# The layer-0 input stage of a two-layer trunk: pooled pieces stored one hook later, and two kinds of stores issued by another engine

## The chip, the cores and the metric

One core of a Trainium2 chip runs one program. The metric is device time in microseconds (us): the median of several executions. A profile is one execution of its own, recorded by the hardware profiler; its times are us from the first instruction.

## The reference, cut to what matters

The program is one inference step of a trunk of two layers on 2048 sample tokens and 128 context tokens of width 1024. Layer 0 modulates and normalises the tokens, projects them into six parts, and mixes two branches:

```python
q_lat, kv_lat, k_pe, gate_a, pool_in, gate_b = jnp.split(h @ w_in, SPLITS_AB, axis=-1)
q = (rmsnorm(q_lat, q_norm) @ w_uq).reshape(B, T, MLA_HEADS, QK_NOPE + QK_ROPE)
...
for g, w in enumerate(POOL_WINDOWS):      # 2, 4, 8, 16 tokens, four groups of 128 channels
    mean = (csg[:, hi] - csg[:, lo]) / (hi - lo)
    d = mean - uf[:, :, sl]
    outs.append(d @ w_pool[g])
o_b = jnp.concatenate(outs, axis=-1) * pool_scale
mixed = jnp.concatenate([o_a * jax.nn.silu(gate_a), o_b * jax.nn.silu(gate_b)], axis=-1)
```

The change touches only how the pooling branch and the q products are carried through memory in layer 0's input stage.

## The kernel before

**Stages.** The input stage of layer 0 is the first quarter of the program (about 60 to 500 us), then come attention and the rest. It walks over five blocks of tokens (512, 512, 512, 384 and 256 wide, blocks 0 to 4). Per block, TensorE (PE) makes products against pairs of weight tiles: `kv` (one pair), `q` (one pair), then `pool`, `gb` and `ga` (two pairs each; block 0 has `gb`, `ga`, `pool`). A pair fills one of two PSUM buffers `psA`, so PE cannot start the pair after next before the buffer is read out.

**Weights.** `wload` (L421 to L424) loads a raw tile `r` from memory by a transfer that SP issues, ScalarE (ACT) casts it to the high part (L423), and VectorE (DVE) subtracts for the low part (L160). Every product is three matmuls (L177 to L179). A `w` in a row is such a tile; four raw tiles exist at a time.

**Evacuation.** `evac_consume` reads a finished pair with one ACT activation (L592, SiLU or copy) and stores it by `store_pair` to `up_d`, `gb_d` or `ga_d` in memory; `store` (one line, L167 in the trace) picks the issuing queue by a letter: 's' is SP, 'a' ACT. The q products are split by an ACT cast (L562, high part, stored by `ST_QH`) and a DVE subtract (low part, `ST_QL`) into `q_d`; the rope part (L492 to L495 on DVE, cast L579) goes out by `ST_QP`.

**Hooks.** After each pair of `pool`, `gb` and `ga` the program writes a hook: one step of each of some generators. 'n' prepares the next block (L333, L295, then L357 and L351 on DVE and L361 on ACT: the modulated tokens `h`), 'l' is a quarter of the modulation vector (four L266 on DVE, from a raw tile `r` of `w_ada_T` by SP), 'p' is a step of the pooling of the block before.

**Pooling.** For each of four channel groups (`gi` 0 to 3) `pool_sums` loads `u` from `up_d` and `gt` from `gb_d` into tiles `pl` (four buffers in all), POOL (GpSimd) makes the window sums (L640, then L644 up to three times for `gi` 3), and `gate` scales on DVE (L654, L656) and stores to `mix_d` (by SP). Before, one hook step is the gate and the store of one group, and at once the loads and sums of the next.

**Order.** Each engine and each queue runs its instructions in the order in which the program writes them, as far as the framework's scheduler leaves it. A load on SP that waits for a buffer holds everything behind it on SP.

Of the kernel before, what the change touches and what calls it, by code (L numbers as in the profile page):

```python
# [65 lines left out]
POOL_AT = 0  # L66
POOL_Y = 0
ST_POOL = 's'
ST_EV = 's'
ST_QH = 's'  # L70
ST_QL = 's'
ST_QP = 's'
ST_X = 'g'
# [40 lines left out]
def trunk_kernel(ctx, tc, xT, cols_in, cond_in, ident_in, edge_in, rope_in, w_ada, w_ada_T, w_in_t, w_inp_T, w_pool,  # L114
# [41 lines left out]
    def f(ap):  # L156
        return ap.bitcast(F32)
# [8 lines left out]
    def store(c, *a):  # L166
        qs[c].dma_start(*a)  # L167
# [39 lines left out]
    mix_d = dram.tile([8, P, T], F32, name="mix_d")  # L207
# [325 lines left out]
    def q_consume(bi, ps, tab):  # L533
# [19 lines left out]
        for hp in range(2):  # L553
# [11 lines left out]
            for a in range(2):  # L565
                store(ST_QH, q_d[2 * hp + a, :, 0, o:o + n], f(th[:, a, :n]))
                store(ST_QL, q_d[2 * hp + a, :, 1, o:o + n], f(tl[:, a, :n]))
# [17 lines left out]
    def store_pair(dst, i, o, n, t):  # L585
        store(ST_EV, dst[i:i + 2, :, o:o + n].rearrange("g p n -> p g n"), t[:, :, :n])

# [22 lines left out]
    def pooling(t0, t1, lo_t, hi_t, alloc=pool_tiles, size=PT):  # L610

        m = -(-(t1 - t0) // size)
        cuts = [t0 + (t1 - t0) * i // m for i in range(m + 1)]
        for a, b in zip(cuts[:-1], cuts[1:]):
            yield from pool_piece(a, b, lo_t, hi_t, alloc)

    def pool_piece(t0, t1, lo_t, hi_t, alloc):
        for gi in range(4):
            gate = pool_sums(gi, t0, t1, lo_t, hi_t, alloc)
            yield  # L620
            gate()
            if POOL_Y:
                yield

    def pool_sums(gi, t0, t1, lo_t, hi_t, alloc):

        w = WINDOWS[gi]
        n = t1 - t0
        L = n + 16
        u, gt, cur, other = alloc()  # L630
        a, b = max(t0 - 8, lo_t), min(t1 + 8, hi_t)
        c0 = a - (t0 - 8)
        if c0:
            G.memset(u[:, :c0], 0.0)
        c1 = c0 + b - a
        if c1 < L:
            G.memset(u[:, c1:L], 0.0)
        store(LD_POOL, u[:, c0:c1], up_d[gi, :, a:b])
        store(LD_POOL, gt[:, :n], gb_d[gi, :, t0:t1])
        G.tensor_tensor(out=cur[:, 1:L], in0=u[:, 0:L - 1], in1=u[:, 1:L], op=ALU.add)  # L640
        a0, a1, step = 1, L, 1
        while 2 * step < w:
            b0, b1 = a0 + step, a1 - step
            G.tensor_tensor(out=other[:, b0:b1], in0=cur[:, b0 - step:b1 - step],  # L644
                            in1=cur[:, b0 + step:b1 + step], op=ALU.add)
            cur, other = other, cur
            a0, a1, step = b0, b1, 2 * step
        if t0 == lo_t:
            G.tensor_tensor(out=cur[:, 8:16], in0=cur[:, 8:16], in1=edge[:, gi, 0:8], op=ALU.mult)
        if t1 == hi_t:  # L650
            G.tensor_tensor(out=cur[:, n:n + 8], in0=cur[:, n:n + 8], in1=edge[:, gi, 8:16], op=ALU.mult)

        def gate():
            V.scalar_tensor_tensor(out=cur[:, 8:8 + n], in0=cur[:, 8:8 + n], scalar=1.0 / w,  # L654
                                   in1=u[:, 8:8 + n], op0=ALU.mult, op1=ALU.subtract)
            V.scalar_tensor_tensor(out=cur[:, 8:8 + n], in0=cur[:, 8:8 + n],  # L656
                                   scalar=cols[:, C_PS + gi:C_PS + gi + 1],
                                   in1=gt[:, :n], op0=ALU.mult, op1=ALU.mult)
            store(ST_POOL, mix_d[4 + gi, :, t0:t1], cur[:, 8:8 + n])
        return gate  # L660

    def head_loads():
        uq, uk, up = ht(F32, (P, 4, 256)), ht(F32, (P, 4, P)), ht(F32, (P, 2, 2, P))
# [593 lines left out]
    def last_pooling():  # L1257
        todo = []
        for t0, t1, lo_t, hi_t in ((BLOCKS[-1][0] - 8, DEC, 0, DEC), (DEC, T, DEC, T)):
            for gi in range(4):  # L1260
                todo.append(pool_sums(gi, t0, t1, lo_t, hi_t, pool_tiles_late))
                if len(todo) > 2:
                    todo.pop(0)()
                yield
        for gate in todo:
            gate()
    pools = last_pooling()
    finishing = []
    g.gated = None
# [159 lines left out]
```

## Time and profile before

| | |
|---|---|
| median of 3 runs | 2059.51 us (2058.22 to 2059.84) |
| the profiled execution | 2053.45 us, of which 2051.7 us is the span |
| PE busy | 1986.3 us, 97% of the span, mean granted clock 0.993 |
| DVE, ACT, POOL busy | 1467.2, 1108.1, 581.3 us |

The profiled execution is 6.06 us below the median of the runs, so sums are made against 2053.45 us and carried over to the median as a difference. PE is busy nearly all the time; what can be gained or lost is in its 65 us of waits and in the stretches in which its clock is low.

### The profile page before, as it was taken

How to read it: one execution, taken by the hardware profiler on the slowest of the kernel's cores; microseconds unless marked ns; L12 is line 12 of the kernel's file. 1: busy time of each engine (PE TensorE's matmuls, PEld its weight loads, DVE VectorE, ACT ScalarE, POOL GpSimd, SP SyncE). 2: the span in 40 equal slices, each digit the busy share in tenths (PEclk: the TensorE clock that was granted, in tenths of full speed). 3: DMA queues.
4: the chain of work that ended last, by engine and by line, in shares of the span. 5: the costliest groups of instructions: out<-in, count | busy, mean ns of one | idle time of the engine just before them, and what ended most of it. 6: DMA issues, size and time to landing. Idle time of an engine off the chain costs nothing.

```text
span 2051.7 us, 26144 instructions
## 1 busy us (share of the span) xinstructions
PE 1986.3 (97%) x9652; PEld 1661.7 (81%) x9652; DVE 1467.2 (72%) x2222; ACT 1108.1 (54%) x1301; POOL 581.3 (28%) x405
## 2 busy tenths in 40 slices
PE   6999898999999999999999999999999999999997
PEld 3787787998777777777758788888889888889987
DVE  4698887765888888888884997455665566577575
ACT  4644344544676767676754635442454335535554
POOL 1002111111478787878762110001001110010000
PEclk9999999999999999999999999999999999999999
DMA  9587777676111010101135553344434542464463
GB/s 362 186 271 244 259 219 244 193 240 195 51 32 52 27 51 29 49 30 49 36 125 174 184 206 124 123 136 152 164 100 137 184 148 89 134 226 154 131 228 124
DMA packets 123696, 300.62 MB, mean 147 GB/s; under 512 B 12144, under 2 KB 39088, under 8 KB 123568
## 3 DMA queue, kind: packets, MB, share of 16 engines
q1 hardware_dynamic: 105168, 258.58, 38.2%
q10 hardware_dynamic: 13728, 23.60, 3.7%
q0 software_dynamic: 4672, 16.78, 2.3%
q8 instruction: 76, 1.25, 0.3%
q14 instruction: 52, 0.43, 0.1%
HBM read 243.23 MB, written 55.67 MB: 146 GB/s over the span
## 4 chain that ended last, share of the span: by engine, by line
PE 78%; DVE 9%; DMA 4%; issue 3%; ACT 3%; POOL 1%; SPq 1%; DVEq 0%; ACTq 0%; POOLq 0%
PE psA L177 17%; PE psA L178 17%; PE psA L179 17%; PE psA L821 3%; PE psA L822 3%; PE psA L823 3%; PE psA L824 3%; PE psA L825 3%; PE psB L178 2%; PE psB L179 2%; PE psB L177 2%; PE psB L917 2%; DVE w L160 1%; DMA r<-wp_d 1%; PE psB L1173 1%
## 5 line engine op out<-in xcount | busy, mean ns | idle before, releaser
L177 PE MATMUL psA<-h,w 128*128 128x512 f32 (+2 forms) x1600 | 578.3, 362 | 17.8 <-ACT e L592 16.1
L179 PE MATMUL psA<-h,w 128*128 128x512 f32 (+2 forms) x1600 | 574.0, 359 | 0.0
L160 DVE TENSOR_TENSOR w<-r,w 128x1024 fp32r<-128x1024 f32 x280 | 351.8, 1260 | 296.3 <-PE psA L178 199.8
L178 PE MATMUL psA<-h,w 128*128 128x512 f32 (+2 forms) x1536 | 550.0, 358 | 1.1 <-DVE h L160 1.1
L423 ACT CAST w<-r 128x1024 fp32r<-128x1024 f32 x280 | 291.9, 1049 | 253.2 <-PE psA L179 172.8
L177 PEld LDWEIGHTS psA<-h,w 128*128 128x128 f32 x1600 | 303.7, 190 | 58.8 <-ACT e L592 17.9
L179 PEld LDWEIGHTS psA<-h,w 128*128 128x128 f32 x1600 | 303.5, 190 | 38.3 <-issue 0.2
L178 PEld LDWEIGHTS psA<-h,w 128*128 128x128 f32 x1536 | 291.9, 190 | 37.7 <-DVE h L160 2.2
L874 POOL TENSOR_TENSOR w<-h,w 128x1024 fp32r<-128x1024 f32 x105 | 252.4, 2417 | 104.6 <-ACT w L872 101.3
L846 DVE TENSOR_TENSOR run<-psA,run 128x512 f32<-128x512 f32 x240 | 163.8, 683 | 42.1 <-ACT h L836 38.3
L836 ACT COPY h<-psA 128x1024 f32<-128x1024 f32 (+1 forms) x145 | 139.4, 962 | 78.2 <-PE psA L825 78.0
L868 ACT ACTIVATE h<-h 128x1024 f32<-128x1024 f32 (+1 forms) x145 | 143.4, 1011 | 64.0 <-DVE h L866 63.8
L866 DVE TENSOR_TENSOR h<-h,psC 128x1024 f32<-128x1024 f32 (+1 forms) x145 | 163.7, 1147 | 0.7 <-PE psC L860 0.7
L178 PE MATMUL psA<-o,w 128*128 128x512 f32 (+2 forms) x368 | 134.0, 366 | 0.0
L887 POOL TENSOR_TENSOR e<-e,h 128x512 f32<-128x512 f32 x92 | 120.8, 1313 | 5.3 <-ACT h L868 0.5
L872 ACT CAST w<-h 128x1024 fp32r<-128x1024 f32 x105 | 110.5, 1052 | 4.1 <-PE psB L179 3.1
L179 PE MATMUL psA<-o,w 128*128 128x512 f32 (+2 forms) x304 | 109.1, 361 | 0.0
L177 PE MATMUL psA<-o,w 128*128 128x512 f32 (+2 forms) x304 | 108.9, 361 | 0.0
L177 PE MATMUL psA<-w,h 128*128 128x512 f32 x272 | 106.7, 393 | 1.6 <-ACT o L1149 1.6
L640 POOL TENSOR_TENSOR pl<-pl 128x527 f32<-128x527 f32 (+2 forms) x16 | 18.8, 1177 | 308.7 <-DMA pl<-up_d 227.1
L178 PE MATMUL psA<-w,h 128*128 128x512 f32 x272 | 106.0, 390 | 0.1
L179 PE MATMUL psA<-w,h 128*128 128x512 f32 x272 | 105.9, 390 | 0.0
(298 smaller groups left out, 3543.2 us busy)
## 6 DMA issues: line engine op xcount, KB each, us to landing
r<-in_w_inc_t_dram SPq DMA_DIRECT2D x80, 512.0 KB, 3.5
r<-in_w_in_t_dram SPq DMA_DIRECT2D x60, 512.0 KB, 4.3
r<-in_w_oap_t_dram SPq DMA_DIRECT2D x40, 512.0 KB, 3.5
r<-in_w_incv_t_dram SPq DMA_DIRECT2D x40, 512.0 KB, 4.2
r<-in_w_outc_t_dram SPq DMA_DIRECT2D x40, 512.0 KB, 3.4
r<-in_w_ada_T_dram SPq DMA_DIRECT2D x32, 512.0 KB, 4.4
r<-wp_d SPq DMA_DIRECT2D x20, 512.0 KB, 5.6
h<-in_w_ada_dram SPq DMA_DIRECT2D x16, 512.0 KB, 10.2
```

Source lines behind the costliest of these rows:

```text
L160: eng.tensor_tensor(out=out, in0=a, in1=f(hi), op=ALU.subtract)
L177: PE.matmul(ps, w[0], x[0], start=first, stop=False)
L178: PE.matmul(ps, w[0], x[1], start=False, stop=False)
L179: PE.matmul(ps, w[1], x[0], start=False, stop=last)
L423: S.copy(hi, raw)
L836: S.copy(s[:, :nt], ps[:, :nt])
L846: V.tensor_tensor(out=b.max, in0=ps[:, a], in1=s[:, 0] if p == 0 else b.max, op=ALU.max)
L866: V.tensor_tensor(out=s[:, :nt], in0=s[:, :nt], in1=b.m[:, None, :].broadcast_to([P, nt, QB]), op=ALU.subtract)
L868: S.activation(out=s[:, :nt], in_=s[:, :nt], func=AF.Exp, scale=SM_SCALE)
L872: S.copy(ph[:, :nt], s[:, :nt])
L874: low = behind(G.tensor_tensor(out=pl[:, :nt], in0=s[:, :nt], in1=f(ph[:, :nt]), op=ALU.subtract), g.gated)
L887: behind(G.tensor_tensor(out=b.pool[:, 0], in0=b.pool[:, 0], in1=s[:, a], op=ALU.add), low or g.gated)
```

## The change

`ST_EV` and `ST_QH` go from 's' to 'a': the 30 stores of evacuated pairs and the 20 stores of q high parts are issued by ACT and no longer by SP (SP then has 601 rows in place of 651). And a group's pooling is in three steps: sums, gate, store. The store of a group, and with it the loads and sums of the next group, comes one hook behind its gate. What `drain(pools)` finds left at a block's end runs there. `last_pooling`, the pooling of the last tokens, calls the gate and the store together as before.

```diff
@@ -66,8 +66,8 @@
 POOL_AT = 0
 POOL_Y = 0
 ST_POOL = 's'
-ST_EV = 's'
-ST_QH = 's'
+ST_EV = 'a'
+ST_QH = 'a'
 ST_QL = 's'
 ST_QP = 's'
 ST_X = 'g'
@@ -616,11 +616,11 @@
 
     def pool_piece(t0, t1, lo_t, hi_t, alloc):
         for gi in range(4):
-            gate = pool_sums(gi, t0, t1, lo_t, hi_t, alloc)
+            gate, out = pool_sums(gi, t0, t1, lo_t, hi_t, alloc)
             yield
             gate()
-            if POOL_Y:
-                yield
+            yield
+            out()
 
     def pool_sums(gi, t0, t1, lo_t, hi_t, alloc):
 
@@ -656,8 +656,7 @@
             V.scalar_tensor_tensor(out=cur[:, 8:8 + n], in0=cur[:, 8:8 + n],
                                    scalar=cols[:, C_PS + gi:C_PS + gi + 1],
                                    in1=gt[:, :n], op0=ALU.mult, op1=ALU.mult)
-            store(ST_POOL, mix_d[4 + gi, :, t0:t1], cur[:, 8:8 + n])
-        return gate
+        return gate, lambda: store(ST_POOL, mix_d[4 + gi, :, t0:t1], cur[:, 8:8 + n])
 
     def head_loads():
         uq, uk, up = ht(F32, (P, 4, 256)), ht(F32, (P, 4, P)), ht(F32, (P, 2, 2, P))
@@ -1260,10 +1259,12 @@
             for gi in range(4):
                 todo.append(pool_sums(gi, t0, t1, lo_t, hi_t, pool_tiles_late))
                 if len(todo) > 2:
-                    todo.pop(0)()
+                    for it in todo.pop(0):
+                        it()
                 yield
-        for gate in todo:
-            gate()
+        for its in todo:
+            for it in its:
+                it()
     pools = last_pooling()
     finishing = []
     g.gated = None
```

The diff says little of where the rows end up, so three places are shown. The first is SP's queue in block 1, while the sums of that block's last group run (`r` from `in_w_in_t` are weights, from `in_w_ada_T` modulation; `e` evacuated tiles; `pl` pooling tiles). Before:

```order
L167 DMA r341_1748<-in_w_ada_T_dram 128x1024
L167 DMA pl320_1631<-gb_d_100 128x504
L167 DMA mix_d_102<-pl301_1530 128x504
L167 DMA pl423_2161<-up_d_99 128x528
L167 DMA up_d_99<-e315_1610 128x2x512
L421 DMA r346_1758<-in_w_in_t_dram 128x1024
L421 DMA r349_1764<-in_w_in_t_dram 128x1024
```

Now the same weights, there r346 and r349, are r342 and r345:

```order
L421 DMA r320_1625<-in_w_in_t_dram 128x1024
L167 DMA mix_d_102<-pl298_1518 128x504
L167 DMA pl334_1720<-gb_d_100 128x504
L167 DMA pl376_1957<-up_d_99 128x512
L421 DMA r323_1631<-in_w_in_t_dram 128x1024
L167 DMA r337_1730<-in_w_ada_T_dram 128x1024
L167 DMA pl377_1958<-gb_d_100 128x504
L421 DMA r342_1740<-in_w_in_t_dram 128x1024
L421 DMA r345_1746<-in_w_in_t_dram 128x1024
```

The load of pl423, which belongs to the next piece, stood directly ahead of the weights and is now eight rows behind them (it follows r385); the two `up_d` stores are on ACT.

The second place is DVE where block 0 ends: L266 of the modulation tile r251, w234 and w237 are weights, e241 the square sums of the next block. Before:

```order
L160 TENSOR_TENSOR w234_1220<-r232_1216,w233_1218 128x1024
L656 SCALAR_TENSOR_TENSOR pl258_1319<-pl258_1319,cols_81,pl257_1318 128x504
L160 TENSOR_TENSOR w237_1226<-r235_1222,w236_1224 128x1024
L160 TENSOR_TENSOR e241_1281<-e240_1279,e241_1281 128x512
L266 SCALAR_TENSOR_TENSOR psB252_1309,asum_96<-r251_1307,silb0_748 128x512
L266 SCALAR_TENSOR_TENSOR psE254_1313,asum_96<-r251_1307,silb1_749 128x512
L266 SCALAR_TENSOR_TENSOR psB253_1311,asum_96<-r251_1307,silb2_750 128x512
L333 TENSOR_TENSOR e246_1292<-e246_1292,e247_1294 128x1024
L266 SCALAR_TENSOR_TENSOR psE255_1315,asum_96<-r251_1307,silb3_751 128x512
```

Now:

```order
L266 SCALAR_TENSOR_TENSOR psB252_1309,asum_96<-r251_1307,silb0_748 128x512
L266 SCALAR_TENSOR_TENSOR psE254_1313,asum_96<-r251_1307,silb1_749 128x512
L160 TENSOR_TENSOR e202_1100<-e201_1095,e202_1100 128x512
L160 TENSOR_TENSOR w234_1220<-r232_1216,w233_1218 128x1024
L266 SCALAR_TENSOR_TENSOR psB253_1311,asum_96<-r251_1307,silb2_750 128x512
L266 SCALAR_TENSOR_TENSOR psE255_1315,asum_96<-r251_1307,silb3_751 128x512
L654 SCALAR_TENSOR_TENSOR pl258_1319<-pl258_1319,pl256_1317 128x504
L656 SCALAR_TENSOR_TENSOR pl258_1319<-pl258_1319,cols_81,pl257_1318 128x504
L160 TENSOR_TENSOR w237_1226<-r235_1222,w236_1224 128x1024
L160 TENSOR_TENSOR e241_1281<-e240_1279,e241_1281 128x512
L333 TENSOR_TENSOR e246_1292<-e246_1292,e247_1294 128x1024
```

All four L266 of r251 have moved from behind the row of e241 to ahead of it. On SP the load of r251 went from behind the q_d stores, rope and token loads to ahead of them.

The third place is DVE where block 2 ends: pl620 (before) and pl644 (now) are the gates of group 2, pl636 and pl678 those of group 3, L492 to L495 rope, and w554 and w557 the low weights of the two tiles of block 3's kv pair. Before:

```order
L160 TENSOR_TENSOR w554_2822<-r552_2818,w553_2820 128x1024
L654 SCALAR_TENSOR_TENSOR pl620_3181<-pl620_3181,pl618_3179 128x512
L656 SCALAR_TENSOR_TENSOR pl620_3181<-pl620_3181,cols_81,pl619_3180 128x512
L492 STREAM_SHUFFLE e541_2776<-e540_2774 128x512
...
L494 TENSOR_TENSOR e543_2788<-e543_2788,e398_2058 128x512
L160 TENSOR_TENSOR w557_2828<-r555_2824,w556_2826 128x1024
L495 TENSOR_TENSOR e543_2788<-e543_2788 128x512
L654 SCALAR_TENSOR_TENSOR pl636_3277<-pl636_3277,pl633_3274 128x512
L656 SCALAR_TENSOR_TENSOR pl636_3277<-pl636_3277,cols_81,pl634_3275 128x512
```

Now:

```order
L654 SCALAR_TENSOR_TENSOR pl644_3363<-pl644_3363,pl642_3361 128x512
L656 SCALAR_TENSOR_TENSOR pl644_3363<-pl644_3363,cols_81,pl643_3362 128x512
L160 TENSOR_TENSOR w554_2819<-r552_2815,w553_2817 128x1024
L654 SCALAR_TENSOR_TENSOR pl678_3592<-pl678_3592,pl675_3589 128x512
L656 SCALAR_TENSOR_TENSOR pl678_3592<-pl678_3592,cols_81,pl676_3590 128x512
L492 STREAM_SHUFFLE e537_2762<-e536_2760 128x512
...
L494 TENSOR_TENSOR e539_2774<-e539_2774,e398_2058 128x512
L160 TENSOR_TENSOR w557_2825<-r555_2821,w556_2823 128x1024
L495 TENSOR_TENSOR e539_2774<-e539_2774 128x512
```

The gate of group 3 stood behind the whole rope and w557 and is now ahead of both. The end of block 3 reads in the same way (pl785 ahead of the rope and of w684, where pl749 stood behind them). In block 2 itself the gate of group 3 (rows 291 and 296 of DVE's order, in the run between L333 and L357) is now at rows 264 and 274, where that of group 2 was.

## Rows read from the trace of the kernel before

**Rows 1.** waits of PE, 60 to 500 us: us in total, times, longest

```profile
PE psA L177 <- ACT e L592: 16.1, 4, 6.2
```

**Rows 2.** timeline of PE's four waits: start, length, operation, [idle before <-releaser]

```profile
184.75 0.47 PE L319 MATMUL psD<-e,ones 128*128 128x512 f32 x1 [2.11 <-DVE e L295]
...
218.78 0.80 PE L177 MATMUL psA<-h,w 128*128 128x512 f32 x1 [6.23 <-ACT e L592]
...
324.39 0.79 PE L177 MATMUL psA<-h,w 128*128 128x512 f32 x1 [6.17 <-ACT e L592]
...
414.27 0.68 PE L177 MATMUL psA<-h,w 128*128 128x384 f32 x1 [3.41 <-ACT e L592]
```

**Rows 3.** windows of 2 us of PE: length, busy (matmuls), granted clock, DMA share, GB/s

```profile
218.00:220.00 2.00, 1.22 (x3) 0.50 0.51 198
220.00:222.00 2.00, 2.00 (x7) 0.50 1.02 380
222.00:224.00 2.00, 2.00 (x8) 0.71 0.90 277
224.00:226.00 2.00, 2.00 (x11) 1.00 0.95 349
```

**Rows 4.** timeline of SP's queue behind the pooling store, block 1

```profile
198.23 0.33 SPq L167 DMA_DIRECT2D mix_d<-pl  x1
207.09 0.32 SPq L167 DMA_DIRECT2D pl<-up_d  x1
...
207.98 2.25 SPq L421 DMA_DIRECT2D r<-in_w_in_t_dram  x2
```

**Rows 5.** timeline of POOL, ACT and DVE in the same place

```profile
202.87 4.19 POOL L644 TENSOR_TENSOR pl<-pl 128x517 f32<-128x517 f32 x3 [3.13 <-DMA mix_d<-pl]
...
214.11 1.04 ACT L423 CAST w<-r 128x1024 fp32r<-128x1024 f32 x1 [3.89 <-DMA r<-in_w_in_t_dram]
...
217.70 1.02 ACT L592 ACTIVATE e<-psA 128x1024 f32<-128x1024 f32 x1
...
211.85 1.40 DVE L357 SCALAR_TENSOR_TENSOR h<-h,amul,e 128x512 f32<-128x512 f32 x2
```

**Rows 6.** timelines of SP and DVE ahead of it, block 0's end

```profile
145.64 7.82 SPq L167 DMA_DIRECT2D q_d<-e  x8
...
156.75 0.70 SPq L167 DMA_DIRECT2D r<-in_w_ada_T_dram  x1
...
165.51 0.70 DVE L266 SCALAR_TENSOR_TENSOR psB<-r,silb 128x512 f32<-128x512 f32 x1 [2.24 <-DMA r<-in_w_ada_T_dram]
```

**Rows 7.** timelines of ACT and DVE ahead of the second wait, block 2

```profile
320.86 1.14 ACT L361 ACTIVATE h<-h,mod 128x384 fp32r<-128x384 f32 x2 [1.58 <-DVE h L357]
...
303.28 0.63 DVE L654 SCALAR_TENSOR_TENSOR pl<-pl,pl 128x512 f32<-128x512 f32 x1
...
307.55 0.75 DVE L656 SCALAR_TENSOR_TENSOR pl<-pl,cols,pl 128x512 f32<-128x512 f32 x1
```

**Rows 8.** timelines of DVE, POOL and PE where blocks 2 and 3 end

```profile
356.91 0.75 DVE L656 SCALAR_TENSOR_TENSOR pl<-pl,cols,pl 128x512 f32<-128x512 f32 x1
...
364.31 2.07 DVE L160 TENSOR_TENSOR w<-r,w 128x1024 fp32r<-128x1024 f32 x1
...
362.45 5.09 POOL L644 TENSOR_TENSOR pl<-pl 128x525 f32<-128x525 f32 x3
...
364.73 0.33 PE L177 MATMUL psA<-h,w 128*128 128x384 f32 x1
364.90 0.34 PE L178 MATMUL psA<-h,w 128*128 128x384 f32 x1
```

**Rows 9.** landings of the pooling store, an issue on ACT, busy us in 100 to 500

```profile
mix_d<-pl SPq DMA_DIRECT2D x8, 256.0 KB, 3.5
...
554.94 0.35 ACTq L167 DMA_DIRECT2D e<-ga_d  x1
...
sum 400.00, PE 381.59 PEld 334.79 DVE 310.09 ACT 183.19 POOL 53.19; mean PE 95.40 PEld 83.70 DVE 77.52 ACT 45.80 POOL 13.30
```

## The prediction

> **What bounds the kernel now.** I read the page first: PE is busy 97% of the span, so only its waits and its slow-clock stretches can pay or cost. Everything that the change touches lies in layer 0's input stage, so next came the waits of PE there [rows 1] and PE's timeline at them [rows 2]. The reader is to see four waits and one kind: PE waits 6.23 us at 218.78, 6.17 at 324.39 and 3.41 at 414.27 for the activation L592 that empties `psA`, once in each of blocks 1 to 3, and 2.11 us at 184.75 for DVE's L295. That is 17.9 us. Behind each the granted clock is at its lower level: 0.50, 0.50 and 0.71 in three windows of 2 us behind the first, with 7 and 8 matmuls where 11 fit at 1.00 [rows 3]. Seven matmuls lost, at 2/11 us each, are 1.3 us. So about 1 to 1.5 us goes with a wait; for all four some 5 us. The most that the stage can give is 23 us, 1.1% of the time.
>
> Then the question for each wait is what its L592 waited for.
>
> *First wait.* ACT runs in order. L592 at 217.70 stands behind a table load, two L361 and the weight cast L423, which began at 214.11 after 3.89 us of waiting for its load of `r` [rows 5]. That load left SP at 207.98, behind a pooling load of `u` issued at 207.09 [rows 4]. SP's last issue before that was at 198.23, so it stood 8.5 us: the buffer came free only when POOL had ended three L644, begun at 202.87 and 4.19 us long, because they themselves wait for the landing of the store of 198.23 [rows 4, 5]. But DVE limits the same place: L361 needs L357, and the pair of L357 of 211.85 ends at 213.25 [rows 5]. From the cast's end (215.15) to L592 two L361 and a table load take 2.55 us. Had the weights been there, these would have run from 213.25, and L592 at 215.8 in place of 217.70. So SP alone is worth 1.9 us here; the rest hangs on DVE.
>
> *Second wait.* At 320.86 ACT waits 1.58 us for L357, no load is in it [rows 7]: DVE alone sets it. The third wait has the same form.
>
> **The change part by part.**
>
> *Weights ahead of the pooling load, block 1.* The order of SP shows the `u` load that stood for 8.5 us (pl423) behind the weights. The store of a piece, and the sums that wait for it, come a hook later. That gives the 1.9 us above.
>
> *The modulation load at block 0's end.* It left SP at 156.75 because eight q_d stores, which occupy SP's queue for 7.82 us, stood ahead, and an `up_d` store and others behind them; DVE then waited 2.24 us for it at 165.51 [rows 6]. Now it is ahead of the q_d stores. The four L266 (0.70 each and what follows: 2.6 us) leave the stretch in which DVE has no gap, and the wait goes with them, though some of the 2.24 us is taken up by the square sums' own inputs. I take 3.0 of the 4.8 us. DVE then ends L357 at 210.2, L592 can run at 212.8, and the wait falls by 1.9 + 3.0 to 1.3 us: **-5.0**, rounded, and with it the low clock's share of the place, **-1.2** (bounds: -2.5 if little of DVE's gain arrives, -7.5 if all of wait and clock goes). The wait of 2.11 us before it has DVE's same lateness and I give it **-0.8** (0 to -2.1).
>
> *Block 2.* A gate moves out of DVE's dense run ahead of L592: L654 and L656, 0.63 and 0.75 us [rows 7]; the stretch begins a little earlier because SP has one store fewer ahead of its weights, some 0.8 us. **-2.2** (-1.0 to -3.5). Block 3 has no gate in that run in either order: 0.
>
> *The gate of group 3 ahead of the rope, blocks 2 and 3.* This is the price. Before, the gate of group 2 ended at 357.66, the rope and the low weights of w557 followed, ending at 366.38, and the sums of group 3 ran beside them (three L644, 5.09 us). PE's kv pair began at 364.73, its matmuls stand 0.17 us apart, so its second tile, which needs w557, begins 24 matmuls later at 368.9 [rows 8]: 2.5 us to spare. Now DVE stands at the gate of group 3 with rope and w557 behind it. That gate needs the store of group 2 landed (3.5 us [rows 9]) and three L644. In block 1 such a three took 4.19 us [rows 5]. So from the end T of the gate of group 2: 0.2 + 3.5 + 4.2 + 1.4 for the gate itself, then 6.8 for rope and w557 without POOL beside them (8.7 before, an estimate from the seven rope rows at 0.7 and a subtract at 1.2, plus gaps), which makes T + 16.1 against 368.9. T can be 357.7 as before, and w557 is 4.9 us late; or as early as 352.7 or so, since the gates are now spread over more hooks, and nothing is late. I take T near 354, 1.0 us late, and 1.0 for the clock. Block 3 has the same order with narrower tiles; I take the same. Sum **+4.0**, bounds 0 and +13 (twice 4.9 and 1.5).
>
> *The issues on ACT.* 50 stores; one issue on ACT took 0.35 us, which makes 17.5 us spread over 440 us on an engine that is busy 45.8% there [rows 9]. Each follows the activation that made its data, so it waits for little; the cast behind it is what could be late, and the L592 of the three waits has no store ahead of it in its run. **0** (to +2 if a store stands for its semaphore ahead of a cast that matters).
>
> Sum: -5.0 - 1.2 - 0.8 - 2.2 + 4.0 + 0 = -5.2 us. From 2053.45 us that is 2048.3 us; the median of the runs lies 6.06 us above the profiled execution, so the forecast is 2059.5 - 5.2 = **2054.3 us**. A measurement tells about 0.2% from no change, 4.1 us, so this is faster by a little more than can be told.
>
> The Trainium skill (DMA: Bandwidth & Descriptors, Issuing engines are not separate DMA queues) says that transfers issued by several engines run on the same 16 DMA engines, so that spreading the issues saves only the sequencer's time. This trace agrees on the size of an issue (0.35 us on ACT, 0.32 on SP). What it doesn't cover is the 8.5 us that a load stood, which is a matter of order in one queue.
>
> **The rivals.**
>
> *No change: only issue time is saved.* The stores leave SP, but SP isn't what the L592 wait for: blocks 2 and 3 wait for L357 on DVE [rows 7], and in block 1 DVE's own limit lies 1.9 us below. If DVE doesn't start earlier, -1.9 and -1.4 for one gate, with the new gate order at +2, leave -1.3: 2058.2 us. For it: three of four waits end with DVE. Against it: DVE's wait of 2.24 us sits behind an SP queue that the change empties. Taken to its end, the rule of the Trainium skill named above (same page and section) gives this case too, at 2059.5 us.
>
> *A trade.* The four gains come, and the gate of group 3 is late by 3 us in each of two blocks, with 1.5 of clock: -9.2 + 9.0, 2059.3 us. Same by measurement, by another way.
>
> *Slower: DVE stands behind POOL at the kv pairs.* T stays at 357.7 in block 2 and as late in block 3, w557 comes 4.9 us late, 6.4 with the clock; if POOL is as slow as beside a busy DVE (5.09 in place of 4.19) 7.3. Twice 7.3 less 9.2 is +5.4: 2064.9 us. It decides from 6.7 us a place on (13.3 in all). For it: DVE's row order is certain. Against it: DVE idles before the old gates of groups 1 and 2, so T has room to come earlier.
>
> **How the numbers follow.** Forecast as above (faster, between 2048 and 2055.4): 0.47. The trade, with its neighbours: 0.16; no change: 0.13, so 0.29 within 0.2%. Slower: 0.24. The range reaches from all of the first waits' gains with no price, -9.2 and some more clock, 2048.5, to the slower rival, 2065.0; what is left out on each side is about one in ten. The forecast's own range is 2048.5 to 2057.
>
> **What would show it.** In the profile after: the wait at 218.78 at 1 to 3 us with ACT's cast there not waiting for a load; DVE's 2.24 us wait for the modulation tile gone; SP's 8.5 us stand no longer ahead of weights; the wait at 324.39 near 4 us, that at 414.27 unchanged. New: DVE idle 5 us or more at L654 with POOL's L644 as releaser at the ends of blocks 2 and 3, and perhaps waits of PE for DVE's w near 369 and 448. If those PE waits exceed 5 us each the prediction is wrong to the slow side; if DVE reaches the first L357 no earlier than before, it is wrong because the gain never was SP's.

## The result, and the profile after

The changed kernel takes 2069.1 us (median of 6 runs, 2064.84 to 2071.23) against 2058.86 us beside it: a ratio of 1.0055, 95% interval 1.0042 to 1.0068 (the two medians alone give 1.0050, inside it). It is slower. The forecast was 2054.3 us with a range to 2065.0, so the time lies outside the range, on the other side of no change.

The page of the changed kernel (busy us, share of the span, instructions):

```profile
span 2069.5 us, 26128 instructions
...
PE 1993.9 (96%) x9652; PEld 1665.6 (80%) x9652; DVE 1463.0 (71%) x2222; ACT 1109.7 (54%) x1301; POOL 580.6 (28%) x405
```

No engine has more work to speak of. Its waits of PE in 60 to 500 us (in total, times, longest):

```profile
PE psA L177 <- ACT e L592: 14.3, 5, 4.9
PE psD L319 <- DVE e L295: 5.0, 2, 3.8
PE psB L701 <- DMA e<-in_w_inp_T_dram: 4.5, 3, 2.3
PE psA L179 <- DVE w L160: 2.7, 3, 1.4
PE psD L320 <- DVE e L160: 1.8, 1, 1.8
```

The waits for L592 fell from 16.1 us in four [rows 1] to 14.3 in five. The others grew, and their places are in PE's timeline:

```profile
105.59 1.13 PE L701 MATMUL psB<-pl,e 128*128 128x128 f32 x8 [1.80 <-DMA e<-in_w_inp_T_dram]
118.12 0.50 PE L177 MATMUL psA<-h,w 128*128 128x512 f32 x1 [2.54 <-ACT e L592]
180.59 0.50 PE L179 MATMUL psA<-h,w 128*128 128x512 f32 x1 [1.38 <-DVE w L160]
192.55 0.47 PE L319 MATMUL psD<-e,ones 128*128 128x512 f32 x1 [1.23 <-DVE e L295]
223.70 0.79 PE L177 MATMUL psA<-h,w 128*128 128x512 f32 x1 [4.94 <-ACT e L592]
288.98 0.50 PE L320 MATMUL psD<-e,ones 128*128 128x512 f32 x1 [1.76 <-DVE e L160]
304.17 0.47 PE L319 MATMUL psD<-e,ones 128*128 128x512 f32 x1 [3.82 <-DVE e L295]
335.10 0.69 PE L177 MATMUL psA<-h,w 128*128 128x512 f32 x1 [3.27 <-ACT e L592]
380.12 0.44 PE L179 MATMUL psA<-h,w 128*128 128x384 f32 x1 [0.50 <-DVE w L160]
425.93 0.45 PE L177 MATMUL psA<-h,w 128*128 128x384 f32 x1 [3.29 <-ACT e L592]
460.79 0.39 PE L179 MATMUL psA<-h,w 128*128 128x256 f32 x1 [0.80 <-DVE w L160]
```

The rows at 192.55, 223.70, 335.10 and 425.93 answer to the four of [rows 2]: 1.23 for 2.11, 4.94 for 6.23, 3.27 for 6.17, 3.29 for 3.41. The rows at 380.12 and 460.79 are the kv pairs of the forecast's price.

Both programs issue the same matmuls in the same order (but for 23 rows near 100 us, where sixteen L701 and seven rows of the next pair have changed places), so the n-th of one trace can be held against the n-th of the other. I call the difference of their starts the *delay of PE*. At the places that stood at 142, 250, 330 and 530 us before, the changed kernel is 7.0, 5.5, 10.2 and 14.0 us late. Stretch by stretch that is +7.0 in block 0, -1.5 in block 1, +4.7 from block 1's end through block 2, +3.8 over the kv pairs and behind. (From 530 us to the end 3.4 more come; single executions differ by as much there. The profiled run of before is itself 6 us below its median.) The forecast has terms for the second stretch (-7.0), the third (-2.2) and the fourth (+4.0), and none for block 0.

At the end of block 1 one chain is to be seen whole. Timelines of DVE, SP's queue and ACT there in the changed kernel:

```profile
255.17 0.69 DVE L654 SCALAR_TENSOR_TENSOR pl<-pl,pl 128x512 f32<-128x512 f32 x1 [2.32 <-POOL pl L644]
...
263.33 1.45 DVE L266 SCALAR_TENSOR_TENSOR psB<-r,silb 128x512 f32<-128x512 f32 x1 [3.71 <-DMA r<-in_w_ada_T_dram]
...
269.56 0.69 DVE L495 TENSOR_TENSOR e<-e 128x512 f32<-128x512 f32 x1
...
256.68 0.33 SPq L167 DMA_DIRECT2D mix_d<-pl  x1
257.82 0.33 SPq L167 DMA_DIRECT2D r<-in_w_ada_T_dram  x1
...
270.93 3.30 SPq L167 DMA_DIRECT2D q_d<-e  x4
...
275.49 1.05 SPq L421 DMA_DIRECT2D r<-wp_d  x2
...
282.75 1.05 ACT L423 CAST w<-r 128x1024 fp32r<-128x1024 f32 x1 [9.99 <-DMA r<-wp_d]
```

DVE waits 2.32 us at the gate for POOL's sums. The store of the piece leaves SP behind that gate, the modulation load behind the store, and the first L266 that needs this load stands in the middle of the rope and waits 3.71 us. So the rope ends at 270.25, its q_d stores and the weights behind them on SP come late, and ACT's cast of these weights begins at 282.75; in the trace of before it begins at 271.47. That is 11.3 us later, of which PE's delay of 5.5 us at the start of this stretch explains half. PE pays at 288.98 (1.76 us) and 304.17 (3.82 us). But that one place doesn't carry the whole loss, as the runs show.

### The profile page after: what moved, and what is told of

It is laid out like the page before. It is cut to its first block, busy times and chain, and to the rows that moved or that the text cites. A ratio compares the mean times of both kernels' runs of the same rounds, so it can differ in the third digit from the quotient of the medians.

```text
span 2069.5 us, 26128 instructions
## 1 busy us (share of the span) xinstructions
PE 1993.9 (96%) x9652; PEld 1665.6 (80%) x9652; DVE 1463.0 (71%) x2222; ACT 1109.7 (54%) x1301; POOL 580.6 (28%) x405
## 4 chain that ended last, share of the span: by engine, by line
PE 66%; DVE 6%; DMA 3%; issue 2%; ACT 2%; POOL 2%; SPq 1%; ACTq 0%; DVEq 0%; POOLq 0%
PE psA L178 13%; PE psA L177 13%; PE psA L179 13%; PE psA L820 3%; PE psA L821 3%; PE psA L822 3%; PE psA L823 3%; PE psA L824 3%; PE psB L178 2%; PE psB L179 2%; PE psB L177 2%; PE psB L916 2%; DVE w L160 1%; PE psB L1172 1%; PE psE L1172 1%
## 5 line engine op out<-in xcount | busy, mean ns | idle before, releaser
L177 PE MATMUL psA<-h,w 128*128 128x512 f32 (+2 forms) x1600 | 577.9, 361 | 15.9 <-ACT e L592 14.3
L177 PEld LDWEIGHTS psA<-h,w 128*128 128x128 f32 x1600 | 304.0, 190 | 56.9 <-ACT e L592 16.1
L845 DVE TENSOR_TENSOR run<-psA,run 128x512 f32<-128x512 f32 x240 | 164.1, 684 | 42.6 <-ACT h L835 38.9
## 6 DMA issues: line engine op xcount, KB each, us to landing
h<-in_w_ada_dram SPq DMA_DIRECT2D x16, 512.0 KB, 10.2
```

Of the source, the lines that this page charges most:

```text
L177: PE.matmul(ps, w[0], x[0], start=first, stop=False)
L845: V.tensor_tensor(out=b.max, in0=ps[:, a], in1=s[:, 0] if p == 0 else b.max, op=ALU.max)
```

## The experiments

Ratios are to the kernel before, run on the same chip in the same session of measuring, with 95% intervals. The sessions of the experiments ran on four chips.

**Each part of the change alone.**

```diff
 # pool_only: the changed kernel
-ST_EV = 'a'
-ST_QH = 'a'
+ST_EV = 's'
+ST_QH = 's'
 # stores_only: the kernel before with both at 'a'; ev_only and qh_only: with one of them
```

> The pooling in three steps, with all 50 stores back on SP. Theory A (the stores on ACT change the order of what stays on SP: in block 0 a modulation load ahead of the third load of w_inp_T, at block 1's end a pooling store ahead of a modulation load; these two places cost the 5 and 8 us): here neither order is there, so no slower than before, ratio 0.997 to 1.001, no wait of 1.8 us at the third L701 group, no DVE wait over 1 us for a modulation tile inside the rope of block 1. Theory B (the store of a piece one hook later is what puts it in front of the modulation load): ratio 1.004 to 1.006, with DVE's 3.7 us wait inside the rope still there.

> Both kinds of stores on ACT, pooling as before. Theory A: ratio 1.004 to 1.007, block 0 loses its 5 us by 118 us, and DVE waits 2 us or more for a modulation tile inside the rope at block 1's end. Theory B: block 0 loses 5 us but block 1's end loses nothing, ratio 1.001 to 1.003.

> Only the 30 stores of evacuated pairs on ACT. Its order on SP and DVE at the two places is that of both kinds moved, so theory A says the same ratio as with both, within 0.002. A third theory, C (the issues on ACT themselves delay its casts), says in between: 30 of 50 issues, some 60% of the loss.

> Only the 20 stores of q high parts on ACT. Theory A: again the ratio of both kinds moved, within 0.002, as the order at the two places is the same. Theory C: 40% of the loss.

| run | ratio |
|---|---|
| `pool_only`, three pooling steps alone | 0.9996 (0.9987 to 1.0005) |
| `stores_only`, 50 stores on ACT | 1.0082 (1.0065 to 1.0100) |
| `ev_only`, the 30 of evacuated pairs | 1.0067 (1.0054 to 1.0079) |
| `qh_only`, the 20 of q's high parts | 0.9996 (0.9988 to 1.0005) |

The pooling steps alone change nothing, and most of the loss comes with `ST_EV`. Twenty stores on ACT cost nothing (for `qh_only` I had misread the order: at the two places it stands as before). Thirty of another kind cost 0.67%. Theory C falls, since its 40% of the loss is not in `qh_only`. Theory B falls by the ratio of `pool_only`, but one of its signs is there and theory A missed it: DVE waits 3.08 us for a modulation tile at 251.18, inside the rope of block 1, in a kernel that loses nothing. `stores_only` lies above theory A's 1.007. The Trainium skill (DMA: Bandwidth & Descriptors, Issuing engines are not separate DMA queues) has it that spreading issues saves only the sequencer's time. `qh_only` agrees, at 0.9996; `ev_only`, at 1.0067, does not, and the question was what else moved.

**Undoing single places of the new order.** Theory A held that two places carry the loss: the third `w_inp_T` load behind a modulation load in block 0 (PE waits at 105.59), and L266 inside the rope (above).

```diff
 # inp_pool: POOL issues the w_inp_T loads
-            dma(wi, w_inp_T[gi].rearrange("p (k n) -> p k n", k=8))
+            G.dma_start(wi, w_inp_T[gi].rearrange("p (k n) -> p k n", k=8))
 # rope_first: L266 may not stand ahead of the rope's last operation (g.roped, set at L495)
-                        V.scalar_tensor_tensor(out=ps1("BE"[a]), ...
+                        behind(V.scalar_tensor_tensor(out=ps1("BE"[a]), ..., g.roped)
 # both: the two together;  ev_undone: the changed kernel with ST_EV = 's'
```

> The changed kernel with the four loads of w_inp_T issued by POOL, which does nothing in block 0, in place of SP. If the 5 us of block 0 are the third such load standing behind a modulation load that waits for its buffer (theory A, first place), the waits at the third L701 group and at the L592 of 118 us shrink from 1.8 and 2.5 us to under 1, the delay against before at 140 us falls from 7 to 3 us or less, and the ratio from 1.0055 to about 1.003. If the loss there is the ACT stores themselves (theory C), nothing changes: 1.0055.

> The changed kernel with an issue order that keeps every L266 behind the rope that the program wrote before it. If block 1's end loses because DVE stands inside the rope at an L266 whose load left SP behind a pooling store (theory A, second place), the 3.7 us wait inside the rope is gone, the first weights from wp_d are issued at least 4 us earlier against the kv pair, the waits of 1.8 and 3.8 us near 289 and 304 are under 2 us in sum, and the ratio falls by 0.002 to 0.003, to about 1.003. If it is the gates ahead of the rope (DVE behind POOL, the slower rival of the prediction), only those 2.3 us matter and the ratio stays at 1.005 or above.

> Both edits of the two runs before in the changed kernel. Theory A, both places: ratio 0.998 to 1.002, the loss gone. If the two orders are symptoms and the cause is elsewhere, above 1.003.

> The changed kernel with the 30 stores of evacuated pairs back on SP; pooling in three steps and the q high parts on ACT stay. Theory A: both orders that cost are made by these 30 stores, so ratio 0.998 to 1.001. If the three-step pooling and moved stores of any kind cost together, 1.002 or more.

`inp_pool` measures 1.0049 (1.0029 to 1.0068), `rope_first` 1.0046 (1.0030 to 1.0061), `both` 1.0045 (1.0030 to 1.0060), `ev_undone` 1.0024 (1.0014 to 1.0035). Theory A falls as the whole cause. Its first place falls by its own sign: in `inp_pool` PE waits 1.80 us at 105.59 as in the changed kernel, now for ACT's L361, and is 7.9 us late at 142 where 3 or less was expected. `ev_undone` has no pair store on ACT and keeps 0.24%, as the other branch of its expectation has it, though that is no more than sessions differed by (below). In `rope_first` DVE's wait inside the rope is gone, but DVE now waits 29.5 us for POOL's sums in 140 to 400 us, where the changed kernel has 19.2. The scheduler makes another order for each edit: 321 of DVE's 2222 places in `rope_first` hold another operation than in the changed kernel. So I stopped editing the program and fixed the order.

**The order by itself.** The changed kernel and `pool_only` issue the same instructions; only the letters of `ST_EV` and `ST_QH` differ, and the scheduler's order. The edit records each instruction as it is written and ties each of the first 900 on DVE to its predecessor in a list (other engines up to the same point):

```diff
-    V, S, G, PE = nc.vector, nc.scalar, nc.gpsimd, nc.tensor
+    V, S, G, Y, PE = Rec(nc.vector), Rec(nc.scalar), Rec(nc.gpsimd), Rec(nc.sync), nc.tensor
...
+def pin(engines, behind):
+    for c, numbers in PINNED.items():
+        row = [engines[c].did[f"I-{n}"] for n in numbers.split() if f"I-{n}" in engines[c].did]
+        for a, b in zip(row, row[1:]):
+            behind(b, a)
```

`pin_v` is the changed kernel with `pool_only`'s order on DVE, `mir_v` is `pool_only` with the changed kernel's order on DVE; in `pin_all` and `mir_all` the order on ACT, POOL and SP is tied as well, for what both kernels have there. The traces show that the lists took hold: DVE's 2222 operations stand in `pin_v` as in `pool_only` and in `mir_v` as in the changed kernel, and in `pin_all` and `mir_all` so do those of ACT and POOL and the 539 SP transfers that store neither pairs nor q. In their rows all but PE's instructions have the line of the recording helper, L1439.

> The changed kernel, its 50 stores on ACT, with the order of the kernel that has the three pooling steps alone (stores on SP, measured 0.9996) written out for DVE, ACT's own operations, POOL and the SP transfers that both have. Theory D (the loss is the order that the scheduler makes of DVE and the queues once the stores have moved; the issues themselves cost nothing): 0.9996 of the time before, 0.998 to 1.0015. Rival E (issuing by ACT costs by itself, by issue time or by stores that wait in ACT's queue): 1.004 to 1.006, as the changed kernel.

> The changed kernel with DVE's order alone taken from the kernel with the three pooling steps alone; ACT and SP stay free (26 and 93 places there differ from that kernel). Theory D in its strict form (DVE's order carries the loss, by stands at the pooling gates and modulation loads): 0.998 to 1.0015. Rival F (SP's order carries it, loads of weights behind other loads): 1.004 to 1.006. Rival E: 1.004 to 1.006.

> The mirror: the kernel with the three pooling steps alone, its 50 stores on SP, with the changed kernel's order written out for DVE, ACT, POOL and the SP transfers that both have. Theory D: the loss comes back without a store on ACT, 1.0055, 1.004 to 1.008 (more than the changed kernel if SP's stores stand in the way too). Rival E: 0.9996, to 1.001.

> The mirror for DVE alone: the kernel with the three pooling steps alone, stores on SP, with the changed kernel's order on DVE only. Strict theory D: 1.004 to 1.008. Rival F (SP's order): 0.999 to 1.0015. Rival E: 0.9996, to 1.001.

| DVE's order | stores on SP | stores on ACT |
|---|---|---|
| of `pool_only` | 0.9996 (`pool_only`) | 0.9970, 0.9958 to 0.9983 (`pin_v`); 0.9971, 0.9960 to 0.9982 (`pin_all`) |
| of the changed kernel | 1.0167, 1.0153 to 1.0181 (`mir_v`); 1.0111, 1.0097 to 1.0125 (`mir_all`) | 1.0055 (the changed kernel) |

Read down a column, the stores stay and DVE's order changes: it costs 1.7% with the stores on SP (1.15% by `mir_all`) and 0.85% with them on ACT (0.55% by `pin_again`, below). Read along a row, the order stays and the stores move to ACT: the time falls, by 0.26% (not firm, see `pin_again`) in one order and by 1.1% in the other, of which 0.56% is left when the order of ACT, POOL and SP is held too (`mir_all`). The two unpinned cells come from other sessions than the pinned ones; the effects of the lower row and of the left column are larger than the 0.3% by which sessions differed (below). So ACT's issues cost nothing that shows, in either order, and rival E falls. The list for DVE is enough to bring the loss and to take it away.

Rival F (SP's order carries the loss) is not separated by these runs. In `pin_v` the free engines moved with DVE's list: 97 of those 539 SP transfers stand elsewhere than in the changed kernel, and so do 43 of ACT's operations and the 23 rows of PE near 100 us. And SP's order does count: `mir_v` and `mir_all` have the same order on DVE, and with ACT and SP free the ratio is 1.0167 in place of 1.0111, in one session. The prices in both rows came out larger than expected, and `mir_v` larger than the changed kernel. PE's waits in `mir_v`, 60 to 500 us, and three rows of its timelines of DVE and PE:

```profile
PE psA L179 <- DVE w L1439: 32.0, 6, 13.6
PE psA L177 <- ACT e L1439: 7.3, 5, 2.8
```

```profile
388.84 0.69 DVE L1439 SCALAR_TENSOR_TENSOR pl<-pl,pl 128x512 f32<-128x512 f32 x1 [10.50 <-POOL pl L1439]
...
396.47 0.69 PE L179 MATMUL psA<-h,w 128*128 128x384 f32 x1 [13.64 <-DVE w L1439]
...
480.47 0.58 PE L179 MATMUL psA<-h,w 128*128 128x256 f32 x1 [7.85 <-DVE w L1439]
```

This is the forecast's slower rival, at its two places: DVE stands 10.50 us at a gate, the weights and the rope are queued behind it, and the kv pair's `w` comes 13.64 us late. The changed kernel has the same order there on DVE, with its stores on ACT, and pays 0.50 and 0.80. Part of that is the order of ACT and SP: in `mir_all`, which has theirs too, the same gate stands 5.60 us, and the kv pairs pay 3.65 and 3.48. What is left has a row of its own. In `mir_all` the gate of group 0 ends at 355.12 and its pooling store leaves SP 3.9 us later, behind a gb_d store, two loads and two q_d stores:

```profile
358.11 0.80 SPq L1439 DMA_DIRECT2D q_d<-e  x2
358.99 0.41 SPq L1439 DMA_DIRECT2D mix_d<-pl  x1
```

In the changed kernel the gate ends at 347.93 and the store leaves at once:

```profile
347.96 0.33 SPq L167 DMA_DIRECT2D mix_d<-pl  x1
```

The next group's gate stands 8.01 us for POOL in `mir_all` and 4.85 in the changed kernel.

DVE's waits say much the same. Added up over 140 to 400 us, those at the gates (`pl` rows) and those of L266 for modulation loads (`psB` rows):

| kernel | DVE's waits, us | ratio |
|---|---|---|
| `pin_v`, and once more as `pin_again` (below) | 6.9, 6.7 | 0.9970, 1.0000 |
| before | 11.8 | 1 |
| `pool_only` | 21.2 | 0.9996 |
| `qh_only` | 28.8 | 0.9996 |
| `ev_only` | 32.1 | 1.0067 |
| changed | 35.6 | 1.0055 |
| `stores_only` | 38.9 | 1.0082 |
| `ev_undone` | 39.3 | 1.0024 |
| `mir_all` | 43.6 | 1.0111 |
| `mir_v` | 63.1 | 1.0167 |

The runs that are not in the table fit: `pin_all` has 16.0, `seg1` to `seg4` (below) 11.5, 18.3, 17.6 and 25.1, at ratios from 0.9971 to 1.0017, and `inp_pool`, `rope_first`, `both` and `seg24` have 33.1 to 38.9, at 1.0044 to 1.0049. Every kernel up to 28.8 us lies at 1.0017 or below, every one from 32.1 us on at 1.0024 or above. Within the two groups the order of the columns does not always agree; that what a wait costs depends on what is queued behind it is my reading.

**Which places.** `seg1` to `seg4` are `pin_v` with the changed kernel's DVE order put back in one stretch of the list each (instructions 0 to 121, 121 to 237, 237 to 343, 343 to 553). In `seg2` the list begins to differ so (1194 to 1200 are four L266):

```diff
-... 1194 1198 1084 1085 1086 1196 1087 1200 1096 1090 ...
+... 1194 1198 1196 1200 1201 1202 1207 1203 1211 1084 ...
```

> The changed kernel with the DVE order of the run that beat both (pin_v, 2053.6 us), but for its first 121 instructions (to 148 us, block 0), which stand as in the changed kernel. Theory G (the loss is spread; each stretch costs by itself what the delays of PE in the two traces differ by there): +3.7 us, 2057.3. Rival H (one stretch carries nearly all 15 us, the others nothing): 2053.6 or 2068.

> The same with instructions 121 to 237 (148 to 246 us, block 1) as in the changed kernel. Theory G: +6.4 us, 2060.0 (the delay of PE falls by 7.9 us in this stretch in pin_v and by 1.5 in the changed kernel). Rival H: 2053.6 or 2068.

> The same with instructions 237 to 343 (246 to 345 us, from block 1's end through block 2's weights) as in the changed kernel. Theory G: +0.9 us, 2054.5. Theory of the first runs (the modulation load inside the rope there costs 8 us): 2060 or more.

> The same with instructions 343 to 553 (345 to 534 us, the ends of blocks 2 and 3, where the gate of group 3 stands ahead of the rope) as in the changed kernel. Theory G: +3.7 us, 2057.3; the price of +4.0 in the forecast has its place here, the slower rival's +13 too. Rival H: 2053.6 or 2068.

The ratios were 1.0017 (1.0006 to 1.0029), 1.0004 (0.9991 to 1.0016), 0.9993 (0.9979 to 1.0007) and 1.0001 (0.9988 to 1.0014), all above `pin_v` in another session; the excesses add up to 28 us, where the two whole orders differ by 17.5. So the base was run again (`pin_again`, the kernel of `pin_v` unchanged), beside one with the stretches of `seg2` and `seg4` together (`seg24`):

> The kernel of pin_v once more, beside runs of the kernel before on the chip of this call: is it really below both kernels (0.9970 then), or did the four stretch runs sit high because the base does? If the base holds: 0.996 to 0.9985. If it sits 4 us higher with them: 0.9985 to 1.0005.

> The changed kernel with the pinned DVE order, but with two stretches as in the changed kernel: block 1 (148 to 246 us) and the ends of blocks 2 and 3 (345 to 534 us). Theory G (stretches add): by the delays of PE, 5.0 + 4.2 us above pin_again, 1.0045 of it. Rival (a delay in one stretch is taken up by the waits of the next): less than 6 us above it.

`pin_again` measured 1.0000 (0.9987 to 1.0013), and `seg24` 1.0044 (1.0029 to 1.0059). The same kernel was at 0.9970 in one session and at 1.0000 in another, on another chip, with intervals that do not meet: sessions differed by 0.3%, and a single stretch can't be timed across them. That `pin_v` beats the kernel before is therefore not shown. That it beats the changed kernel rests on 1.0055 from a session of its own, against 0.9970 and 1.0000; both gaps are above 0.3%. Within one session, `seg24` lies 0.44% above `pin_again`, 9.1 us, where 9.2 were expected (5.0 and 4.2): the rival that had less than 6 us falls.

What one stretch costs is read from the delay of PE gathered inside it, us. Each list is in several runs, which shows the spread of single executions:

| stretch (us before) | the changed kernel's order there | `pin_v`'s order there |
|---|---|---|
| block 0, to 142 | +7.0 (changed), +4.7 (`seg1`) | +0.2 to +3.3 in six runs |
| block 1, 142 to 250 | -1.5 (changed), -2.4 (`seg2`), -1.3 (`seg24`) | -7.9 to -4.6 in five |
| block 1's end and block 2, 250 to 330 | +4.7 (changed), +4.4 (`seg3`) | +3.4 to +3.8 in six |
| kv pairs, 330 to 530 | +3.8 (changed), +4.3 (`seg4`), +6.3 (`seg24`) | -0.6 to +0.5 in five |

The six runs are `pin_v`, `pin_again` and the four of `seg1`, `seg2`, `seg3`, `seg4` and `seg24` that keep this stretch as it is, in two rows three of them. In no row do the two columns overlap, and each list's mean against the other's gives about 4, 4, 1 and 5 us, 14 in all: the loss is spread, as theory G has it. Rival H falls within one session as well: the four ratios lie within 0.24% of each other, so no stretch stands 0.55% or more above three that cost nothing. The times of the single stretches don't confirm G's sizes: above `seg3`, `seg1` lies 0.24%, `seg2` 0.11% and `seg4` 0.08% (each ratio to about 0.13%), where G has 2.8, 5.5 and 2.8 us, that is 0.14%, 0.27% and 0.14%. How a stretch can cost is plainest in `seg2`, timelines of DVE and PE:

```profile
162.94 0.70 DVE L1439 SCALAR_TENSOR_TENSOR psB<-r,silb 128x512 f32<-128x512 f32 x1 [11.29 <-DMA r<-in_w_ada_T_dram]
...
164.81 1.22 DVE L1439 TENSOR_TENSOR w<-r,w 128x1024 fp32r<-128x1024 f32 x1
...
166.08 0.60 PE L179 MATMUL psA<-h,w 128*128 128x512 f32 x1 [5.01 <-DVE w L1439]
```

The same place on DVE in `pin_again`:

```profile
155.83 1.22 DVE L1439 TENSOR_TENSOR w<-r,w 128x1024 fp32r<-128x1024 f32 x1
...
157.85 2.12 DVE L1439 TENSOR_TENSOR w<-r,w 128x1024 fp32r<-128x1024 f32 x1
...
167.25 0.70 DVE L1439 SCALAR_TENSOR_TENSOR psB<-r,silb 128x512 f32<-128x512 f32 x1 [0.90 <-DMA r<-in_w_ada_T_dram]
```

In `seg2` an L266 stands 11.29 us for its modulation load, and the weights that PE needs are behind it. In `pin_again` they are ahead of it. The changed kernel has DVE's order of `seg2` there and not this wait, since it comes to the place later: its DVE reaches this L266 at 159.45, 4.5 us behind the issue of the load (154.98), and in `seg2` DVE is free for it at 151.65, 3.6 us ahead of the issue (155.24).

## Why the prediction was wrong

By stretches, forecast against the delay of PE in the traces: block 0, 0 against +7.0; block 1, -7.0 against -1.5; block 1's end and block 2, -2.2 against +4.7; kv pairs, +4.0 against +3.8. That is -5.2 against +14.0 in single executions (+10.2 by the medians).

**Two steps failed. The larger is the sum itself: it prices the new order at the three places that had been read, and puts every other place at nothing, without a reason.** Block 0 has +7.0. From 250 to 300 us, at the end of block 1, the delay grows by 8.1 us, of which 3.4 are lost again at the second wait. The runs with written lists show what of this is DVE's order: in block 0 +4.7 and +7.0 against at most +3.3. In the third stretch most of the +4.7 is in `pool_only`'s order too (+3.4 to +3.8); there it came with the pooling steps as much as with the letters, and the sum has neither. How much of the +7.0 is order stays open.

**The other step is "The modulation load at block 0's end": the four L266 "leave the stretch in which DVE has no gap, and the wait goes with them", 3.0 us.** *First wait:* forecast -5.0, measured -1.3 (6.23 to 4.94). The part of SP was right: ACT's cast there now waits 0.39 us for its load in place of 3.89 [rows 5]. The part of DVE failed. The load did go out ahead of the q_d stores, at 154.98. But the next quarter's load followed them, at 167.73, its L266 was drawn into the same stretch, and the wait came back longer. Timelines of DVE and ACT:

```profile
177.56 0.70 DVE L266 SCALAR_TENSOR_TENSOR psB<-r,silb 128x512 f32<-128x512 f32 x1 [4.14 <-DMA r<-in_w_ada_T_dram]
...
179.32 1.22 DVE L160 TENSOR_TENSOR w<-r,w 128x1024 fp32r<-128x1024 f32 x1
...
219.14 1.41 DVE L357 SCALAR_TENSOR_TENSOR h<-h,amul,e 128x512 f32<-128x512 f32 x2
...
216.76 1.06 ACT L423 CAST w<-r 128x1024 fp32r<-128x1024 f32 x1 [0.39 <-DMA r<-in_w_in_t_dram]
```

In place of 2.24 us [rows 6] it is 4.14, and the `w` of 179.32 is the one for which PE waits 1.38 at 180.59. Over 140 to 400 us DVE waits 15.4 us for modulation loads, in place of 5.7. The forecast's own sign of failure came: the L357 that L592 needs is 7.3 us later than before (211.85 to 219.14), where PE was 6.2 us late ahead of it. The gain did exist in another order, and without this step: with `pool_only`'s list block 1 has -4.6 to -7.9, where -7.0 was forecast. In `pool_only` itself the load leaves SP behind the q_d stores as before, L357 comes at 209.60, and the first wait is:

```profile
214.14 0.50 PE L177 MATMUL psA<-h,w 128*128 128x512 f32 x1 [0.97 <-ACT e L592]
```

*The wait of 2.11, block 2, block 3.* The numbers came out: -0.9 for -0.8, -2.9 for -2.2, -0.1 for 0. The first two are luck. Neither place gained: PE came later. At the first of them PE had just lost 1.38 us. At the second the row behind the wait stands 10.7 us later than before (324.39 to 335.10), and PE reached the wait 13.6 us later (318.22 to 331.83). In `pool_only`, which has the same pooling steps, that wait is 7.13 us at 324.98.

*The gate of group 3 ahead of the rope.* The mechanism is as described: DVE stands at L654 for POOL's L644 three times in a row, the gates of groups 1 to 3 of block 2, with the rope and `w` behind them.

```profile
355.32 0.69 DVE L654 SCALAR_TENSOR_TENSOR pl<-pl,pl 128x512 f32<-128x512 f32 x1 [4.85 <-POOL pl L644]
...
364.18 0.69 DVE L654 SCALAR_TENSOR_TENSOR pl<-pl,pl 128x512 f32<-128x512 f32 x1 [5.24 <-POOL pl L644]
364.91 0.75 DVE L656 SCALAR_TENSOR_TENSOR pl<-pl,cols,pl 128x512 f32<-128x512 f32 x1
...
372.44 0.69 DVE L654 SCALAR_TENSOR_TENSOR pl<-pl,pl 128x512 f32<-128x512 f32 x1 [5.65 <-POOL pl L644]
...
378.85 1.21 DVE L160 TENSOR_TENSOR w<-r,w 128x1024 fp32r<-128x1024 f32 x1
```

T, the end of group 2's gate, is 365.66, or 355.5 with PE's delay of 10.2 us taken off (forecast 354); `w` ends at T + 14.4 (forecast T + 16.1). So each kv pair costs about half of its term: the delay grows by 0.8 and 1.1 us there, of the 2.0 forecast for each. That the whole stretch has +3.8, close to the +4.0, is luck. The other 1.9 us come elsewhere between 330 and 530 us; `seg4` and `seg24` show that the stretch costs by DVE's order, not at which rows.

*The issues on ACT.* 0 was right for the issues themselves, by `qh_only` and by the rows of the table of four. What the new letters cost is the order that came with them, and the term has none of it.

*The clock.* A wait's share was read too low. The counts in [rows 3] include matmuls that only reach into a window. By their starts, the ten from 218.78 to 223.20 took 4.4 us, and ten at the full clock behind them 2.3: 2.1 us in place of 1.3. It changes no verdict.

*The rivals.* No change and the trade fell with the size. The slower one named the mechanism (DVE, in order, at a gate with weights behind it), but put it at the kv pairs, where it cost little; it cost at the end of block 1, at a modulation load as much as at a gate. At the places that it named its price exists, 13.64 and 7.85 us, in `mir_v`, with the stores on SP. The range ended at this rival's 2065.0 and left out that the new order could cost at other places too.

## What to carry to other kernels

A change of a letter that moves stores between queues is, under a scheduler, a new order for every engine, and the order can be worth more than the letter. Before the sum is made, go through the whole difference of orders on the engine that is nearly full, and price each instruction that waits on a late input by what is queued behind it. To tell an edit from the order that came with it, fix the order: two orders by two edits make four runs, and each effect is read with the other held. Tie every engine whose order is not the question, and run all four in one session.

## What the runs showed of the hardware that was not expected

Fifty stores issued by ACT, at the same order of DVE, ACT, POOL and the rest of SP, took 0.56% off the time (1.0111 to 1.0055, from two sessions), where DVE waits for POOL's pooling chain: on SP they stood ahead of a pooling store, and the gate behind it stood 8.01 us in place of 4.85. And one program measured 0.9970 and 1.0000 of another in two sessions on two chips, each with an interval of 0.0013 to either side.
